# A diffusion trunk on one core: the convolution layer's modulation maps loaded ahead in a ring, its last rows' convolution maps and centring moved earlier, and the context's squares taken about a seven-tile mean

## The chip, the cores and the metric

The kernel runs on one core of a Trainium2 chip. The metric is the time in microseconds (us) of one execution on the device. Five engines work side by side, each with its own queue in program order: PE (TensorE, matrix products), DVE (VectorE), ACT (ScalarE), POOL (GpSimd) and SP (SyncE, which here only issues transfers). A queue stops at an instruction whose operands are not there yet, and all that stands behind it stops too.

## What is computed

Two layers over 1024 latent tokens and 256 context tokens of width 1024. Layer 0 mixes tokens by a convolution module, layer 1 by attention, and each is followed by a SwiGLU network. This case is about layer 0:

```python
mod_x = silu(c) @ w_mod[i] + b_mod[i]            # six vectors: shift, scale, gate, twice
mod_c = silu(c_ctx) @ w_mod[i] + b_mod[i]
hx = rmsnorm(x, norm_g[i, 0]) * (1.0 + sc_x) + sh_x
hc = rmsnorm(ctx, norm_g[i, 0]) * (1.0 + sc_c) + sh_c

def conv_module(h, ...):                          # for hx and for hc
    u = h @ w_pw1 + b_pw1
    a, gt = split(u, 2); u = a * sigmoid(gt)
    u = depthwise_conv(u, w_dw, width 31) + b_dw
    u = silu(layernorm(u, ln_g, ln_b))            # mean and variance over 1024 features
    return u @ w_pw2 + b_pw2
```

## The kernel before

Features lie on the 128 partitions, in KT = 8 tiles; tokens lie along the free dimension, in three pieces: C (256 context tokens), L and R (512 latent tokens each). A product in full precision is made of three passes (high part times high, high times low, low times high), so a weight tile of 128x1024 is loaded (`wload`), rounded on ACT into `wh` (L142), and its remainder `wl` is made by DVE (L146) or by POOL (L148), as the number `lo_dve` says.

**The beginning.** `build` first needs 16 of the modulation vectors (shift and scale, 8 feature tiles each). `mod_pe(f)` (L234) loads map f, 512 KB, on SP's queue, multiplies it on PE by silu(c) and silu(c_ctx) (L243, 8 products in two passes each, so a pair of maps is 32 rows of the trace), copies the result out on ACT (L246), transposes it (L248) and adds a bias on ACT (L250). The loop over k = 0..7 makes maps k and 8+k and then lets the generators `gC`, `gL`, `gR` go on by a step. Each of these squares the 8 tiles of its piece (ACT L388/L391, DVE L392), forms the row statistic (PE L368, DVE L334 to L342, PE L380) and applies norm, scale and shift tile by tile (DVE L400, ACT L405, DVE L406). The maps lie in ten slots `raws`, in tiles T4, T5 and KB; R's result later takes T4 and T5. Also in this loop: the loads of x for L and R (`load_x`), the row of c, c_ctx for all partitions (`cond_row`, 1 MB, and a silu of 128x2048 on ACT), and the first two weight tiles of `pw1`.

**The middle.** For k = 0..7 `pw1` makes u for the three pieces (L453 to L455, 48 products each) and gates it (L461, L462). `conv` treats 64 groups of 16 channels, q = 8k+g, each as nine products with Toeplitz maps (L531 to L534). `conv_maps` makes the two halves of a group's map on DVE (L505, 128x640 each) into a ring of slots `self.cw` (3, later 6). `modg` is `mod_dve`: the other 24 modulation vectors as reductions on DVE (L273, two for each), a step at two of three turns of the `pw1` loop.

**The end.** After the last `pw1` the remaining groups run. A group's result is taken out by ACT (L535) and DVE (L537); `conv_sum` (L557) adds up 8 groups for the mean. For the last feature tile the results go into the context's buffer by eight transfers of 16 partitions, issued from ACT (L542). Then `ln("C")`: `mean` (DVE L568, PE L570), subtract the mean from the 8 tiles (L592), square and add up (L391, L392), statistic, scale (L604), silu (L607), and the context's `pw2` (L626).

Order on each engine: the program gives a priority to every instruction, and a scheduler at build time fixes each queue.

Of the kernel before, what the change touches and what calls it, by code (L numbers as in the profile page):

```python
# [8 lines left out]
F32 = mybir.dt.float32  # L9
F32R = mybir.dt.float32r  # L10
I32 = mybir.dt.int32
AF = mybir.ActivationFunctionType
ALU = mybir.AluOpType
# [41 lines left out]
class Kern:  # L55
# [175 lines left out]
        self.col = [[{} for s in range(2)] for l in range(2)]  # L231


    def mod_pe(self, f, raw=None, rows=None):  # L234

        nc = self.nc
        out = self.bank("md")
        if raw is None:
            raw = self.raw()
        nc.sync.dma_start(raw, self.a["wmod"][f])  # L240
        with self.later(20):
            for k in range(KT):
                nc.tensor.matmul(out[0:2, 0:P], lhsT=self.cs[:, k, :], rhs=raw[:, k * P:(k + 1) * P],  # L243
                                 start=k == 0, stop=k == KT - 1)
        rows = self.sm(P) if rows is None else rows
        nc.scalar.copy(rows[0:2, :], out[0:2, 0:P])  # L246
        with self.later(40):
            nc.tensor.transpose(out[:, P:P + 2], rows[0:2, :], self.c["ident"][0:2, 0:2])  # L248
        for s in range(2):
            nc.scalar.activation(self.mod[0][s][:, f:f + 1], out[:, P + s:P + s + 1], AF.Identity,  # L250
                                 bias=self.c["bmod"][:, 0, f:f + 1], scale=1.0)
# [258 lines left out]
    def conv(self):  # L510

        nc, c = self.nc, self.c
        for q in range(KT * CG):
# [23 lines left out]
            nc.vector.tensor_tensor(v[:, g, :], v[:, g, :], o[:, OW:2 * OW], op=ALU.add)  # L537
            if g == CG - 1:
                for d, o0, nn in ((self.vc, 0, NC_), (self.vl, 2 + NC_, NL)):
                    if k == KT - 1 and d is self.vc:  # L540
                        for j in range(CG):
                            nc.scalar.dma_start(self.cvs["C"][16 * j:16 * j + 16, k, :], v[:, j, :NC_])  # L542
                    else:
                        nc.scalar.dma_start(d[k].rearrange("g q n -> q g n"), v[:, :, o0:o0 + nn])
                if k == KT - 1:
                    self.load_cv("L", k)
                    self.load_cv("R", k)

                self.conv_sum(v[:, CG // 2:] if k == KT - 1 else v, k)
            elif k == KT - 1 and g == CG // 2 - 1:  # L550
                self.conv_sum(v[:, :CG // 2], k)
            yield

    def conv_sum(self, v, k):
# [3 lines left out]
        if k:  # L558
            nc.vector.tensor_tensor(self.vsum, self.vsum, r, op=ALU.add)

    def mean(self, b):

        nc = self.nc
        ps = self.bank("st")
        if b == "C":
            m = self.sm(CTX)
            mv, shape = m.rearrange("p (s n) -> p s n", n=NC_), [P, PH, NC_]
            nc.vector.tensor_tensor(mv, self.vsum[:, :NC_].unsqueeze(1).to_broadcast(shape),  # L568
                                    self.c["selp"].unsqueeze(2).to_broadcast(shape), op=ALU.mult)
            nc.tensor.matmul(ps[:, :CTX], lhsT=self.c["ones"].to_broadcast([P, P]), rhs=m, start=True, stop=True)  # L570
            return ps
        nn, o, s0 = {"L": (NL, 2 + NC_, 0), "R": (NL, 2 + NC_, 4)}[b]
        for i in range(4):
            nc.tensor.matmul(ps[:, i * nn:(i + 1) * nn], lhsT=self.c["selp"][:, s0 + i:s0 + i + 1].to_broadcast([P, P]),
                             rhs=self.vsum[:, o:o + nn], start=True, stop=True)
        return ps
# [6 lines left out]
    def ln(self, b, stags, box):  # L583

        nc, c = self.nc, self.c
        c0, c1 = PIECES[b]
        n = c1 - c0
        cv = self.cvs[b]
        mean = self.mean(b)[:, :n]
        acc = self.acc(n)  # L590
        for k in range(KT):
            nc.vector.tensor_tensor(cv[:, k, :], cv[:, k, :], mean, op=ALU.subtract)  # L592
            self.sq_acc(acc, cv[:, k, :], k)
            yield
        pb = self.stat(acc, n)
        if b == "C":
            s = self.T(stags[0], [P, KT, n])
            box.append(s)
        else:
            shi, slo = self.halves(*stags, n)  # L600
            box.append((shi, slo))
        for k in range(KT):
            z = cv[:, k, :]
            nc.vector.scalar_tensor_tensor(out=z, in0=z, scalar=c["lng"][:, k:k + 1], in1=pb,  # L604
                                           op0=ALU.mult, op1=ALU.mult)
            if b == "C":
                nc.scalar.activation(s[:, k, :], z, AF.Silu, bias=c["lnb"][:, k:k + 1], scale=1.0)  # L607
                yield
                continue
            nc.scalar.activation(z, z, AF.Silu, bias=c["lnb"][:, k:k + 1], scale=1.0)  # L610
            self.split(shi[:, k, :], slo[:, k, :], z)
            yield
# [361 lines left out]
    def build(self):  # L974
# [20 lines left out]
            col[("sh", 0)] = self.mod[0][s][:, 0:8]  # L995
        raws = [self.T(t, [P, 4, 1024]) for t in ("T4", "T5")] + [self.T("KB", [P, 2, 1024])]
        raws = [raws[i][:, j] for j in range(4) for i in range(3) if j < raws[i].shape[1]]
        for k in range(KT):
            if k == 5:
                self.pre += [self.wload(a["pw1"][0]), self.wload(a["pw1"][KT])]  # L1000
            self.mod_pe(k, raws[2 * k % len(raws)])
            self.mod_pe(8 + k, raws[(2 * k + 1) % len(raws)])
            for s in range(2):
                nc.vector.scalar_tensor_tensor(out=self.col[0][s][0][:, k:k + 1], in0=self.mod[0][s][:, 8 + k:9 + k],
                                               scalar=1.0, in1=c["ng"][:, 0, 0, k:k + 1], op0=ALU.add, op1=ALU.mult)
            if k == 0:
                for _ in range(KT + 1):
                    next(gC)
            if k == 1:
                load_x("L")  # L1010
                self.cond_row(cr)
                for _ in range(KT + 1):
                    next(gL)
                next(gC)
            if k:
                next(gC)
                next(gL)
            if k == 3:
                xs["R"] = self.T("HS", [P, KT, 512])
                load_x("R")  # L1020
                gR = self.norm_in(0, None, (None, "T4", "T5"), *PIECES["R"], hs["R"], xt=xs["R"])
            if k > 3:
                for _ in range(2):
                    next(gR)
        for g in (gC, gL, gR):
            for _ in g:
# [19 lines left out]
        for o, n in ((0, 2), (2 + NC_, 2), (UW - 2, 2)):  # L1046
            nc.gpsimd.memset(self.U[:, :, o:o + n], 0.0)
        modg = self.mod_dve(range(16, 40), cr, (mraw, None), self.ps[:, 5:7].rearrange("p a b -> p (a b)"))
        nc.sync.dma_start(self.craw, a["wwin"][0])
        self.conv_maps()  # L1050
        cg = self.conv()
        for k in range(KT):
            for i, _ in enumerate(self.pw1(k, hs)):
                if k and i == 2:
                    self.split_u(k - 1)
                if k == KT - 1 and i == 4:
                    cw = self.T("T1", [P, 6, NM * P], F32R)
                    self.more_maps([(cw[:, 2 * j], cw[:, 2 * j + 1]) for j in range(3)])
                if 12 * k + i >= 22 and i % 3 != 1:
                    next(cg)  # L1060
                if i % 3 != 2:
                    next(modg, None)
        nc.scalar.activation(self.tiny([P, 16], "nv")[:, :1], c["ones"], AF.Silu)
        for _ in range(4):
            next(cg)
        for g0 in (0, CG // 2):
# [298 lines left out]
```

## Time and profile before

| | us |
|---|---|
| median of three runs | 3011.56 (3008.32 to 3013.97) |
| profiled execution | 3016.96 |
| its span, first to last instruction | 3015.1 |
| PE busy in the span | 2910.9 (97%) |
| DVE, ACT, POOL busy | 1894.4, 1198.0, 246.6 |
| mean granted TensorE clock | 0.982 |

The time of a run is some 2 us longer than the span of its profile. PE is busy nearly throughout, so what matters is where it is not: the first 110 us and the stretch from 363 to 411 us, which are the beginning and the end of the convolution layer.

### The profile page before, as it was taken

The page shows a single profiled execution, that of the slowest core. Times are in us where ns is not written, and L with a number is a line of the kernel's source. Part 1 is how long each engine was busy: PE and PEld are TensorE (multiplying, and loading weights), DVE is VectorE, ACT ScalarE, POOL GpSimd, SP SyncE. Part 2 cuts the span into 40 slices and gives each one's busy share as a digit, 9 for nine tenths or more (in the row PEclk, how much of TensorE's full clock was granted, in tenths as well). Part 3 has the DMA queues.
Part 4 walks back from the last instruction along what each step waited for, and adds up shares of the span by engine and source line. Part 5 has one row for each costly group of instructions (what it writes and reads, how often), then busy time and mean ns, then how long its engine had stood idle before and what let it go on. Part 6 is the DMA issues. An engine that isn't in the chain of part 4 may idle for free. (4 is left out here: it accounts for less than half of the span.)

```text
span 3015.1 us, 39080 instructions
## 1 busy us (share of the span) xinstructions
PE 2910.9 (97%) x15008; PEld 2423.4 (80%) x15008; DVE 1894.4 (63%) x3326; ACT 1198.0 (40%) x1965; POOL 246.6 (8%) x391
## 2 busy tenths in 40 slices
PE   7899979999999999999999999999999999999997
PEld 5788868888888888888888787777787778788886
DVE  5887688856556368333577899666666654743335
ACT  5222256522222235222345788645555543332222
POOL 0000001101022011000013111100000010100000
PEclk9999989999999999999989999989999999999998
DMA  6543344334355234333345211313212243443232
GB/s 238 145 122 82 85 139 140 140 123 141 103 174 187 63 119 152 100 98 98 128 149 154 81 48 45 103 68 88 79 60 81 66 136 98 147 140 97 92 98 63
DMA packets 132299, 336.89 MB, mean 112 GB/s; under 512 B 31504, under 2 KB 53008, under 8 KB 130960
## 3 DMA queue, kind: packets, MB, share of 16 engines
q1 hardware_dynamic: 76432, 221.94, 23.1%
q0 software_dynamic: 29568, 104.36, 10.6%
q10 hardware_dynamic: 26112, 8.10, 1.1%
q8 instruction: 118, 1.93, 0.3%
q14 instruction: 69, 0.57, 0.1%
HBM read 289.76 MB, written 39.19 MB: 109 GB/s over the span
## 5 line engine op out<-in xcount | busy, mean ns | idle before, releaser
L172 PE MATMUL ps<-T,wl 128*128 128x512 f32 (+1 forms) x2032 | 767.6, 378 | 8.4 <-DVE wl L146 8.4
L170 PE MATMUL ps<-T,wh 128*128 128x512 f32 (+1 forms) x2032 | 770.2, 379 | 4.2 <-ACT T L159 2.8
L171 PE MATMUL ps<-T,wh 128*128 128x512 f32 (+1 forms) x1984 | 748.5, 377 | 0.2 <-DVE T L162 0.2
L142 ACT CAST wh<-wr 128x1024 fp32r<-128x1024 f32 x285 | 299.2, 1050 | 766.9 <-PE ps L171 544.2
L146 DVE TENSOR_TENSOR wl<-wr,wh 128x1024 fp32r<-128x1024 f32 x277 | 339.0, 1224 | 295.6 <-ACT wh L142 291.8
L172 PEld LDWEIGHTS ps<-T,wl 128*128 128x128 f32 x2032 | 385.0, 189 | 79.2 <-DVE wl L146 9.7
L170 PEld LDWEIGHTS ps<-T,wh 128*128 128x128 f32 x2032 | 385.1, 190 | 73.1 <-ACT T L159 3.9
L171 PEld LDWEIGHTS ps<-T,wh 128*128 128x128 f32 x1984 | 376.0, 190 | 66.7 <-DVE T L162 1.2
L171 PE MATMUL ps<-HS,wh 128*128 128x512 f32 (+1 forms) x768 | 297.3, 387 | 0.0
L921 DVE TENSOR_TENSOR T<-ps,T 128x512 fp32r<-128x512 f32 x320 | 216.9, 687 | 110.4 <-ACT T L920 109.2
L172 PE MATMUL ps<-HS,wl 128*128 128x512 f32 (+1 forms) x720 | 279.3, 388 | 0.0
L170 PE MATMUL ps<-HS,wh 128*128 128x512 f32 (+1 forms) x720 | 278.9, 389 | 0.0
L920 ACT CAST T<-ps 128x512 fp32r<-128x512 f32 x320 | 185.9, 585 | 193.8 <-PE ps L917 178.4
L917 PE MATMUL ps<-cst,T 128*128 128x128 f32 x1100 | 192.3, 276 | 2.8 <-DVE T L921 2.7
L905 DVE TENSOR_SCALAR_CACHE_REDUCE T<-ps,rq 128x1280 f32<-128x1280 f32 x110 | 170.0, 1545 | 28.5 <-PE ps L899 24.0
L752 DVE TENSOR_TENSOR T<-ps,T 128x512 f32<-128x512 f32 (+1 forms) x168 | 110.6, 664 | 113.1 <-PE ps L172 112.4
L917 PEld LDWEIGHTS ps<-cst,T 128*128 128x128 f32 x1100 | 134.0, 142 | 49.9 <-DVE T L921 29.6
L907 ACT ACTIVATE T<-T,mn 128x1280 f32<-128x1280 f32 x110 | 150.4, 1367 | 56.3 <-DVE T L905 54.4
L727 DVE TENSOR_TENSOR sm<-sm,ps 128x256 f32<-128x256 f32 (+1 forms) x88 | 54.6, 620 | 181.2 <-PE ps L172 181.1
L171 PEld LDWEIGHTS ps<-HS,wh 128*128 128x128 f32 x768 | 144.5, 188 | 28.0 <-DVE HS L162 0.2
L172 PEld LDWEIGHTS ps<-HS,wl 128*128 128x128 f32 x720 | 135.5, 188 | 27.0
L170 PEld LDWEIGHTS ps<-HS,wh 128*128 128x128 f32 x720 | 135.1, 188 | 25.8 <-ACT HS L159 0.8
(240 smaller groups left out, 4678.5 us busy)
## 6 DMA issues: line engine op xcount, KB each, us to landing
wr<-in_w SPq DMA_DIRECT2D x220, 512.0 KB, 3.5
q<-in_w SPq DMA_DIRECT2D x44, 512.0 KB, 3.4
wr<-in_pw SPq DMA_DIRECT2D x35, 512.0 KB, 3.6
HR<-in_wmodT POOLq DMA_DIRECT2D x56, 256.0 KB, 3.9
q<-in_wmodT POOLq DMA_DIRECT2D x56, 256.0 KB, 4.0
q<-qsd POOLq DMA_DIRECT2D x32, 256.0 KB, 3.2
wr<-in_wo SPq DMA_DIRECT2D x16, 512.0 KB, 3.4
qsd<-T POOLq DMA_DIRECT2D x14, 512.0 KB, 3.8
```

What stands on the lines that cost most here:

```text
L142: nc.scalar.copy(hi, raw)
L146: nc.vector.tensor_tensor(lo, raw, hi.bitcast(F32), op=ALU.subtract)
L170: nc.tensor.matmul(out[:, :n], lhsT=wh, rhs=xh, start=k == 0, stop=False)
L171: nc.tensor.matmul(out[:, :n], lhsT=wh, rhs=xl, start=False, stop=False)
L172: nc.tensor.matmul(out[:, :n], lhsT=wl, rhs=xh, start=False, stop=k == nk - 1)
L727: nc.vector.tensor_tensor(h, sa, pb[:, :n], op=ALU.mult)
L752: nc.vector.tensor_tensor(yd, out[:, :c1 - c0], yd, op=ALU.add)
L905: nc.vector.tensor_scalar(out=pt, in0=sc, scalar1=rq[:, h:h + 1], scalar2=None, op0=ALU.mult, op1=ALU.min, accum_out=mn)
L907: nc.scalar.activation(pt, pt, AF.Exp, bias=mn, scale=-1.0, accum_out=sums[:, 0, h:h + 1])
L917: nc.tensor.transpose(tp[:, h * P:(h + 1) * P], Ps[h][:, j * P:(j + 1) * P], c["ident"])
L920: nc.scalar.copy(ph, tp)
L921: nc.vector.tensor_tensor(pl, tp, ph.bitcast(F32), op=ALU.subtract)
```

## The change

- **Maps.** Of the ten slots all are loaded before the loop (after six of them the x of L); inside it each `mod_pe` is followed by the load of the map ten places on. `cond_row` and the loads of `pw1`'s first tiles move to k = 3, `cond_row` behind the x of R. Each generator goes on at other turns. `lo_dve = 1.0` is set before the loop, so POOL makes no remainder here.
- **Middle.** The first taps for `conv_maps` are loaded once R's normalised piece is complete (a copy of one column makes the transfer wait for it). `modg` starts at k = 1.
- **End.** In the last `pw1`, from turn 8 on, three more map slots in T2 (9 in all) and a `conv_maps` at each turn. Transfers of the last tile go out on SP's queue. `shift` estimates the context's mean from seven feature tiles, and `centre` subtracts it from these and adds up their squares during the last groups; when the eighth tile is there, only the small rest of the mean is formed, its square times the number of features is subtracted from the sum of squares, and the rest is subtracted from the tiles. `conv_sum` of the last tile goes in parts of 4, 2 and 2 groups.

```diff
-    def mod_pe(self, f, raw=None, rows=None):
+    def mod_pe(self, f, raw, rows=None):
...
-        nc.sync.dma_start(raw, self.a["wmod"][f])
...
                 for d, o0, nn in ((self.vc, 0, NC_), (self.vl, 2 + NC_, NL)):
+                    eng = nc.sync if k == KT - 1 else nc.scalar
...
-                            nc.scalar.dma_start(self.cvs["C"][16 * j:16 * j + 16, k, :], v[:, j, :NC_])
+                            eng.dma_start(self.cvs["C"][16 * j:16 * j + 16, k, :], v[:, j, :NC_])
...
-                self.conv_sum(v[:, CG // 2:] if k == KT - 1 else v, k)
-            elif k == KT - 1 and g == CG // 2 - 1:
-                self.conv_sum(v[:, :CG // 2], k)
+                self.conv_sum(v[:, CG - 2:] if k == KT - 1 else v, k)
+            elif k == KT - 1:
+                if g == 0:
+                    sh = self.shift()
+                for _ in range(2):
+                    next(sh, None)
+                for g0, g1 in ((0, CG // 2), (CG // 2, CG - 2)):
+                    if g == g1 - 1:
+                        self.conv_sum(v[:, g0:g1], k)
...
+    def by_token(self, v):
+        nc = self.nc
+        ps = self.bank("st")
+        m = self.sm(CTX)
+        mv, shape = m.rearrange("p (s n) -> p s n", n=NC_), [P, PH, NC_]
+        nc.vector.tensor_tensor(mv, v.unsqueeze(1).to_broadcast(shape),
+                                self.c["selp"].unsqueeze(2).to_broadcast(shape), op=ALU.mult)
+        nc.tensor.matmul(ps[:, :CTX], lhsT=self.c["ones"].to_broadcast([P, P]), rhs=m, start=True, stop=True)
+        return ps[:, :CTX]
+
+    def shift(self):
+        nc, cv = self.nc, self.cvs["C"]
+        self.part = self.tiny([P, NC_], "part")
+        nc.vector.tensor_scalar(out=self.part, in0=self.vsum[:, :NC_], scalar1=KT / (KT - 1.0), scalar2=None,
+                                op0=ALU.mult)
+        self.about = self.by_token(self.part)
+        self.cacc = self.acc(CTX)
+        for k in range(KT - 1):
+            self.centre(k)
+            yield
+
+    def centre(self, k):
+        cv = self.cvs["C"][:, k, :]
+        self.nc.vector.tensor_tensor(cv, cv, self.about, op=ALU.subtract)
+        self.sq_acc(self.cacc, cv, k)
...
+        if b == "C":
+            acc, dist = self.cacc, self.tiny([P, NC_], "dist")
+            nc.vector.tensor_tensor(dist, self.vsum[:, :NC_], self.part, op=ALU.subtract)
+            mean = self.by_token(dist)
+            self.centre(KT - 1)
+            sq = self.sb(n)
+            nc.scalar.activation(sq, mean, AF.Square, scale=(D / P) ** 0.5)
+            nc.vector.tensor_tensor(acc, acc, sq, op=ALU.subtract)
...
+        def load_map(i):
+            if i < 2 * KT:
+                nc.sync.dma_start(raws[i % len(raws)], a["wmod"][i % 2 * KT + i // 2])
+        for i in range(len(raws)):
+            if i == 6:
+                load_x("L")
+            load_map(i)
+        self.lo_dve = 1.0
         for k in range(KT):
-            if k == 5:
-                self.pre += [self.wload(a["pw1"][0]), self.wload(a["pw1"][KT])]
-            self.mod_pe(k, raws[2 * k % len(raws)])
-            self.mod_pe(8 + k, raws[(2 * k + 1) % len(raws)])
+            for i in (2 * k, 2 * k + 1):
+                self.mod_pe(i % 2 * KT + k, raws[i % len(raws)])
+                load_map(i + len(raws))
...
-            if k == 1:
-                load_x("L")
-                self.cond_row(cr)
+            if k == 2:
...
             if k == 3:
+                self.pre += [self.wload(a["pw1"][0]), self.wload(a["pw1"][KT])]
                 xs["R"] = self.T("HS", [P, KT, 512])
                 load_x("R")
                 gR = self.norm_in(0, None, (None, "T4", "T5"), *PIECES["R"], hs["R"], xt=xs["R"])
+                self.cond_row(cr)
             if k > 3:
-                for _ in range(2):
+                for _ in range(3 if k < 6 else 2):
                     next(gR)
...
+        nc.vector.tensor_copy(self.craw[:, 0:1], hs["R"][0][1][:, KT - 1, 0:1].bitcast(F32))
         nc.sync.dma_start(self.craw, a["wwin"][0])
...
+                if k == KT - 1 and i >= 8:
+                    if i == 8:
+                        cw = self.T("T2", [P, 6, NM * P], F32R)
+                        self.more_maps([(cw[:, 2 * j], cw[:, 2 * j + 1]) for j in range(3)])
+                    self.conv_maps()
...
-                if i % 3 != 2:
+                if k and i % 3 != 2:
                     next(modg, None)
```

What the change does to the queues, at three places (line numbers of the changed kernel are larger; the operations are told by their tiles).

**SP, the beginning.** `in_wmod` is a map, T_113, T_114 and KB its slots, `in_xT` into T_106 the x of L and into HS the x of R, `in_crow` the row for `cond_row`, `in_pw` a weight tile of `pw1`. Before:

```order
L987 DMA T_106<-in_xT 128x2x512 x4
L254 DMA HR<-in_crow 128x2048
L240 DMA T_114<-in_wmod 128x1024
L240 DMA KB<-in_wmod 128x1024
L240 DMA T_113<-in_wmod 128x1024
L240 DMA T_114<-in_wmod 128x1024
L987 DMA HS<-in_xT 128x2x512 x4
L240 DMA T_113<-in_wmod 128x1024
L240 DMA T_114<-in_wmod 128x1024
L141 DMA wr_74<-in_pw 128x1024
```

Now, from the fourteenth map on:

```order
L1036 DMA T_113<-in_wmod 128x1024
L1036 DMA T_114<-in_wmod 128x1024
L1036 DMA KB<-in_wmod 128x1024
L141 DMA wr_74<-in_pw 128x1024
L141 DMA wr_73<-in_pw 128x1024
L1022 DMA HS<-in_xT 128x2x512 x4
L251 DMA HR<-in_crow 128x2048
L141 DMA wr_74<-in_pw 128x1024
```

All 16 maps now stand ahead of `pw1`'s tiles, of R's x and of the row; before, the last eight stood behind R's x and six of them behind `pw1`'s tiles too.

**ACT, around the last pair of maps.** `mod` adds the bias to the last map's product, `q<-KB` rounds the first taps, `sb<-HS` squares R, `HR<-HR` is the silu of the row, `wh` rounds a weight tile, T_274 and T_283 (before) or T_204 and T_325 (now) are the normalised C and L. Before:

```order
L250 ACTIVATE mod_101<-ps,cst 128x1
L250 ACTIVATE mod_102<-ps,cst 128x1
L391 ACTIVATE sb<-HS 128x512
L405 ACTIVATE T_274<-sb,mod_102 128x256
L405 ACTIVATE T_283<-sb,mod_101 128x512
L391 ACTIVATE sb<-HS 128x512
L159 CAST q<-KB 128x320
```

Now:

```order
L247 ACTIVATE mod_101<-ps,cst 128x1
L247 ACTIVATE mod_102<-ps,cst 128x1
L402 ACTIVATE T_204<-sb,mod_102 128x256
L388 ACTIVATE sb<-HS 128x512
L402 ACTIVATE T_325<-sb,mod_101 128x512
L388 ACTIVATE sb<-HS 128x512
L252 ACTIVATE HR<-HR 128x2048
L142 CAST wh<-wr_74 128x1024
L402 ACTIVATE T_204<-sb,mod_102 128x256
L402 ACTIVATE T_325<-sb,mod_101 128x512
```

The row's silu and the rounding of the third weight tile now stand between the last pair of maps and the last tile of C; before, the silu stood far ahead of this place, and the first taps were rounded right behind it.

**DVE, the end of the convolution.** HR gets a group's result, `sm<-HR` is `conv_sum`, KB the context's buffer, `acc` its squares. Before, from the last groups to the statistic:

```order
L537 TENSOR_TENSOR HR<-HR,ps 128x162 x4
L557 TENSOR_REDUCE sm<-HR 128x162
L559 TENSOR_TENSOR HR<-HR,sm 128x162
L568 TENSOR_TENSOR sm<-HR,cst 128x256
L592 TENSOR_TENSOR KB<-KB,ps 128x256 x4
L392 TENSOR_TENSOR acc<-acc,sb 128x256
L592 TENSOR_TENSOR KB<-KB,ps 128x256
```

Now:

```order
L534 TENSOR_TENSOR HR<-HR,ps 128x162 x2
L561 TENSOR_REDUCE sm<-HR 128x162
L563 TENSOR_TENSOR HR<-HR,sm 128x162
L616 TENSOR_TENSOR dist<-HR,part 128x32
L571 TENSOR_TENSOR sm<-dist,cst 128x256
L590 TENSOR_TENSOR KB<-KB,ps 128x256
L389 TENSOR_TENSOR acc<-acc,sb 128x256
L626 TENSOR_TENSOR KB<-KB,ps 128x256
L621 TENSOR_TENSOR acc<-acc,sb 128x256
L626 TENSOR_TENSOR KB<-KB,ps 128x256 x7
L370 TENSOR_SCALAR nv<-ps 128x2
```

Of the eight squares only one is left behind the last group; the eight subtractions are still there, and now stand ahead of the statistic's first row (`nv`). The first `by_token` product stands in PE's queue inside the second group of the last tile.

## Rows read from the trace of the kernel before

**Rows 1.** Stretches of the beginning: from:to in us, its length, then busy us (and instructions) of PE, PE's weight loads, DVE, ACT and POOL, the granted clock, DMA share, GB/s.

```profile
23.00:36.00 13.00, 9.40 (x46) 6.15 (x46) 6.95 (x24) 5.14 (x10) 0.00 (x0) 0.61 1.04 398
91.00:99.40 8.40, 5.76 (x24) 4.36 (x24) 7.17 (x12) 1.73 (x2) 0.00 (x0) 1.00 0.42 125
99.40:106.60 7.20, 6.42 (x27) 5.73 (x28) 5.71 (x9) 0.41 (x1) 0.00 (x0) 0.54 0.85 228
```

**Rows 2.** What PE waited for in the first 440 us: its line, the work that released it, us in total, times, the longest.

```profile
PE ps L243 <- DMA T<-in_wmod: 10.9, 1, 10.9
PE ps L368 <- DVE acc L392: 7.9, 2, 5.6
PE ps L531 <- DVE HR L537: 6.3, 5, 2.8
PE ps L570 <- DVE sm L568: 4.0, 1, 4.0
```

**Rows 3.** PE in order of time: start, us, line, operation, count, and in brackets the idle time before it and what ended it. L243 are the maps, L453 to L455 the products of `pw1`.

```profile
10.93 5.45 PE L243 MATMUL ps<-T,cs 128*2 128x128 f32 x32 [10.93 <-DMA T<-in_wmod]
...
36.70 3.66 PE L243 MATMUL ps<-T,cs 128*2 128x128 f32 x32
...
41.01 3.65 PE L243 MATMUL ps<-T,cs 128*2 128x128 f32 x32
...
48.28 5.32 PE L243 MATMUL ps<-T,cs 128*2 128x128 f32 x32
...
61.64 1.91 PE L243 MATMUL ps<-KB,cs 128*2 128x128 f32 x16
...
90.90 0.50 PE L453 MATMUL ps<-T,wh 128*128 128x512 f32 x1 [1.02 <-DVE HR L462]
...
96.37 0.39 PE L455 MATMUL ps<-T,wl 128*128 128x512 f32 x1
99.41 0.39 PE L453 MATMUL ps<-T,wh 128*128 128x256 f32 x1 [2.65 <-ACT wh L142]
```

**Rows 4.** Transfers of the first 112 us: GB/s in 40 equal slices of 2.8 us, then SP's issue of R's x (start, us), then the longest wait of SP's queue for PE (at L1049, the first taps).

```profile
GB/s 42 343 353 409 391 399 417 405 399 388 390 408 411 407 413 130 4 200 180 0 0 0 0 246 6 59 18 29 0 0 0 0 0 187 187 92 254 219 310 70
...
17.40 5.54 SPq L987 DMA_DIRECT2D HS<-in_xT  x4
...
SPq L1049 <- PE ps L248: 14.0, 1, 14.0
```

**Rows 5.** ACT and DVE in order of time in the beginning: the row's silu, the rounding of a weight tile, a square of R, a remainder, and two runs of R's application.

```profile
26.43 1.89 ACT L255 ACTIVATE HR<-HR 128x2048 f32<-128x2048 f32 x1
43.40 1.03 ACT L142 CAST wh<-wr 128x1024 fp32r<-128x1024 f32 x1
61.90 0.61 ACT L391 ACTIVATE sb<-HS 128x512 f32<-128x512 f32 x1
84.99 2.06 DVE L400 SCALAR_TENSOR_TENSOR sb<-HS,col,ps 128x512 f32<-128x512 f32 x3
86.96 2.07 DVE L406 SCALAR_TENSOR_TENSOR T<-sb,mod,T 128x512 fp32r<-128x512 f32 x3
100.10 1.22 DVE L146 TENSOR_TENSOR wl<-wr,wh 128x1024 fp32r<-128x1024 f32 x1
```

**Rows 6.** The loop over k: when DVE gates R's piece for k = 0, 1 and 7 (L462), and two stretches of one k's length, with and without `modg` (columns as in Rows 1).

```profile
98.30 0.75 DVE L462 SCALAR_TENSOR_TENSOR HR<-ps,cst,sm 128x512 f32<-128x512 f32 x1
...
135.68 0.74 DVE L462 SCALAR_TENSOR_TENSOR HR<-ps,cst,sm 128x512 f32<-128x512 f32 x1
...
364.22 0.75 DVE L462 SCALAR_TENSOR_TENSOR HR<-ps,cst,sm 128x512 f32<-128x512 f32 x1 [1.86 <-ACT sm L461]
...
139.00:177.00 38.00, 38.00 (x226) 34.10 (x225) 33.56 (x51) 8.36 (x15) 0.00 (x0) 1.00 0.46 125
300.00:338.00 38.00, 38.00 (x225) 34.10 (x224) 22.64 (x35) 7.62 (x14) 0.00 (x0) 1.00 0.24 54
```

**Rows 7.** PE at the end of the convolution, in order of time: two groups back to back, a group after a wait, the last group's last product, the mean (L570), the statistic (L368).

```profile
364.55 0.31 PE L531 MATMUL ps<-HS,T 128*128 128x324 f32 x1
...
365.85 0.31 PE L531 MATMUL ps<-HS,T 128*128 128x324 f32 x1
...
386.32 0.42 PE L531 MATMUL ps<-HS,T 128*128 128x324 f32 x1 [2.77 <-DVE HR L537]
...
394.35 0.35 PE L534 MATMUL ps<-HS,T 128*128 128x324 f32 x1
398.66 1.22 PE L570 MATMUL ps<-sm,cst 128*128 128x256 f32 x2 [3.96 <-DVE sm L568]
405.45 1.01 PE L368 MATMUL ps<-cst,acc 128*128 128x1 f32 x4 [5.57 <-DVE acc L392]
```

**Rows 8.** DVE at the end: busy us and count of map halves (L505) in one stretch, then in order of time the sum over eight groups, the sum over four, the last squares, and the context's scaling (L604).

```profile
364.80:398.20 33.40, 15.69 (x20) 0.93 0.66 189
...
382.57 2.49 DVE L557 TENSOR_REDUCE sm<-HR 128x162 f32<-128x1296 f32 x1
...
390.37 1.35 DVE L557 TENSOR_REDUCE sm<-HR 128x162 f32<-128x648 f32 x1
...
403.91 1.48 DVE L392 TENSOR_TENSOR acc<-acc,sb 128x256 f32<-128x256 f32 x3
...
409.61 3.22 DVE L604 SCALAR_TENSOR_TENSOR KB<-KB,cst,ps 128x256 f32<-128x256 f32 x8 [0.78 <-PE ps L380]
```

More of the change, by code (lines that the diff above doesn't have):

```diff
@@ L231, in consts @@
         self.col = [[{} for s in range(2)] for l in range(2)]
-    def mod_pe(self, f, raw=None, rows=None):
+    def mod_pe(self, f, raw, rows=None):
         nc = self.nc
         out = self.bank("md")
-        if raw is None:
-            raw = self.raw()
-        nc.sync.dma_start(raw, self.a["wmod"][f])
         with self.later(20):
@@ L539, in conv @@
                 for d, o0, nn in ((self.vc, 0, NC_), (self.vl, 2 + NC_, NL)):
+                    eng = nc.sync if k == KT - 1 else nc.scalar
                     if k == KT - 1 and d is self.vc:
                         for j in range(CG):
-                            nc.scalar.dma_start(self.cvs["C"][16 * j:16 * j + 16, k, :], v[:, j, :NC_])
+                            eng.dma_start(self.cvs["C"][16 * j:16 * j + 16, k, :], v[:, j, :NC_])
                     else:
-                        nc.scalar.dma_start(d[k].rearrange("g q n -> q g n"), v[:, :, o0:o0 + nn])
+                        eng.dma_start(d[k].rearrange("g q n -> q g n"), v[:, :, o0:o0 + nn])
                 if k == KT - 1:
@@ L564, in mean @@
         ps = self.bank("st")
[L565 to L571, printed above, removed]
         nn, o, s0 = {"L": (NL, 2 + NC_, 0), "R": (NL, 2 + NC_, 4)}[b]
@@ L588, in ln @@
         cv = self.cvs[b]
-        mean = self.mean(b)[:, :n]
-        acc = self.acc(n)
+        if b == "C":
[6 more added lines that the diff above has]
+            nc.vector.tensor_tensor(acc, acc, sq, op=ALU.subtract)
+        else:
+            mean = self.mean(b)[:, :n]
+            acc = self.acc(n)
         for k in range(KT):
             nc.vector.tensor_tensor(cv[:, k, :], cv[:, k, :], mean, op=ALU.subtract)
-            self.sq_acc(acc, cv[:, k, :], k)
+            if b != "C":
+                self.sq_acc(acc, cv[:, k, :], k)
             yield
@@ L1008, in build @@
                     next(gC)
-            if k == 1:
-                load_x("L")
-                self.cond_row(cr)
+            if k == 2:
                 for _ in range(KT + 1):
                     next(gL)
-                next(gC)
-            if k:
-                next(gC)
+            next(gC)
+            if k >= 2:
                 next(gL)
             if k == 3:
+                self.pre += [self.wload(a["pw1"][0]), self.wload(a["pw1"][KT])]
                 xs["R"] = self.T("HS", [P, KT, 512])
@@ L1058, in build @@
                     self.more_maps([(cw[:, 2 * j], cw[:, 2 * j + 1]) for j in range(3)])
+                if k == KT - 1 and i >= 8:
[3 more added lines that the diff above has]
+                    self.conv_maps()
                 if 12 * k + i >= 22 and i % 3 != 1:
                     next(cg)
-                if i % 3 != 2:
+                if k and i % 3 != 2:
                     next(modg, None)
         nc.scalar.activation(self.tiny([P, 16], "nv")[:, :1], c["ones"], AF.Silu)
+        self.banks["st"], self.ring["st"] = [6, 5], 0
         for _ in range(4):
```

## The prediction, made before the changed kernel was run

> **What bounds the kernel now.** I read the shares of busy time first: PE is busy in 97% of the span, so only its waits and its slow stretches can be won. PE's waits of the first 440 us [rows 2] name the places: 10.9 us until the first map lands, and later waits for DVE around the norms, the groups and the mean. The stretches [rows 1] add the clock: from 23 to 36 us PE was busy for 9.4 of 13.0 us at a granted 0.61, a mixture of the levels 1.2 and 2.4 GHz, after idle stretches; from 99.4 to 106.6 it was 0.54, after the 2.65 us in which PE had nothing to do because the weights for k = 1 came late [rows 3]. PE's order in time [rows 3] shows the maps' course: a pair starts at 36.70 and the next at 41.01, so 4.31 us a pair at full clock (3.66 of products, the rest transposes and copies); at the lower level the products of a pair take 5.32. The last map ends near 63.5, with `pw1` products laid between the pairs, and the first R piece ends near 96.7. Transfers run at about 400 GB/s up to 42 us and then nearly stop [rows 4]: the early stretch is filled by bytes that are not all wanted first.
>
> The loop over k is full: R's piece is gated at 98.30, 135.68 and 364.22 us [rows 6], so six k from 1 to 7 take 228.5, 38.1 each. A group costs 1.30 [rows 7], eight are 10.4 to 10.5, so `pw1` itself is 27.6 for one k. The first step of the loop, 98.30 to 135.68, took 37.4 with only one group in it, 28.9 of work: 8.5 were lost there.
>
> At the end, PE has 16 groups left at 363.2, which are 21 us of work, but ends them at 394.7 [rows 7], behind DVE, which makes 20 map halves there for 15.69 us [rows 8] beside gating, splitting and sums. Then the context's mean, squares and statistic run one after another while PE waits 3.96 and 5.57 us [rows 7]; the context's scaling starts at 409.61 [rows 8].
>
> **The change, part by part.** *Maps first.* Ahead of the last map now stand the constants (0.2 MB), C's x (1.05), 16 maps (8.4) and L's x (2.1), 11.8 MB; at the rate of [rows 4] that is some 33 us. PE takes longer: the first pair as before from 10.93 to 16.4, then seven pairs at 4.31 make 46.6, and two norms' statistics and transposes between them about 2, so the last map is through at 48.5, 15 us earlier than now.
>
> A rule of the Trainium skill speaks against the ring: DMA: Bandwidth & Descriptors, in the section on the anatomy of one DMA, says that the engines that move data do not wait on semaphores, so that a transfer's wait is done by the sequencer that issues it; the load of a slot's second map would hold everything behind it on SP. The row agrees: SP stood 14.0 us at L1049 for PE [rows 4]. By that rule the sixteenth map can be issued when the sixth is through, at 27.0 by the pairs above, and R's x, issued at 17.40 before [rows 4], behind it; with 3.7 MB behind that point it lands by 42, or by 44 if the pairs run slower. ACT's queue comes to R's squares at about 47.5 either way; a longer stop of SP is rival (d).
>
> *From the last map to the end of the first R piece.* PE then has 27.6 us of k = 0 and 15 products of C for k = 1 (1.8) in its queue: 77.9 if nothing waited. ACT's queue decides what waits. Between 44 and 59 us it has the two roundings (1.03 each), eight squares of R (0.61), the small copies and biases of the last two pairs, applications for C and L, and then, as the order shows, the row's silu (1.89) and the third rounding [rows 5] ahead of C's last tile. DVE then makes a remainder (1.22) [rows 5], two applications, and R's statistic, which takes 3.2 with its transposes (for the context it is 406.46 to 409.61 [rows 7, 8]); all that ends near 64.9. PE waits there about 2, and about 4 in small pieces before. R's application, with the last two tiles of L and a gating, follows on DVE: 21 instructions at 0.69 (six in 84.99 to 89.03 [rows 5]) up to 79.4; then 23 products of R are left, at 0.24 (24 from 90.90 to 96.77 [rows 3]), 5.4: R ends at 84.8. Before it ended at 96.8. **12 us gained**; bounds: 18 if no wait is left, 4 if all pairs from the fourth run at 1.2 GHz (five times 1.66).
>
> *k = 1.* Its weights are rounded at 59, long before they are needed, and POOL's remainder (PE waited for it) is DVE's now, at 1.22, hidden by the norms. The 8.5 us lost now shrink to about 1, and 1.8 were already done: **9 us gained**; bounds 6 and 10.
>
> *k = 2 to 7.* `modg` leaves k = 0 and is in k = 6. DVE is busy 33.6 of 38 with it and 22.6 without [rows 6]: the eight steps fit. In k = 1 and 2 DVE gets the first maps too, and is filled to about 37 of 38. **0**, bounds 2 either way. Without that cover each microsecond of DVE over PE's 38.1 would count in full.
>
> *The end.* DVE has 14 map halves behind the last gating instead of 20, 0.78 each, 4.7 us less; but `centre` puts five subtractions and as many sums, the first product of a scaled sum, and a reduction of its own before the last group. The first `by_token` product stands in PE's queue inside a group; it needs the sum over k = 6's groups (2.49 [rows 8]) and two short steps, so PE stands there for some 3 to 4 us, where before it stood for 2.77 at about the same work [rows 7]. Counted through DVE's queue from the last gating (364.9 before), the last group ends 28.2 later instead of 29.8. Then the reduction is over two groups, half of the 1.35 for four [rows 8]; ACT's issues of the eight transfers are gone from between its outputs. The mean's product goes off at 31 instead of 33.8. Of the squares one is left, not eight: the sum is ready 2.4 after the product starts, not 6.8; but the eight subtractions, 2.4 more, stand ahead of the statistic, as the order shows. Statistic and transposes as before. The scaling starts at 38.9 instead of 44.7: **6 us gained**; bounds 0, if PE's stop costs the rest of the groups, and 9, if the subtractions hide under the statistic's product. Beyond this place the queues are those of before but for a few rows where attention starts, which I count as 0, one either way.
>
> Sum: 12 + 9 + 0 + 6 = 27. The profiled execution's 3016.96 would be 2990. It stood 5.4 above the median of the runs shown, so the median goes from 3011.56 to **2984.5**. A tenth of a per cent either way is the runs' own scatter; below 0.2% (6 us) I call it no change.
>
> **The rivals.** (a) *The lower clock in the pairs.* From 23 to 36 us the clock fell after short idle stretches; the ring feeds PE without gaps, but copies on ACT still stop it 0.2 to 0.6 us at each pair. If five pairs run at 1.2 GHz, 8 us of the 12 go: 2993. TensorE: Matmul & The Clock Gate, in the section on what is actually happening, in the Trainium skill, has the lower level as the default that activity lifts; the first pair's 5.45 agrees [rows 3].
>
> (b) *The tail moves its wait.* PE's stop inside the last tile, followed by groups at a lower clock, takes all 6: 2990. For it: the groups after 386.32 did start slowly.
>
> (c) *More at the beginning.* If ACT's chain is shorter than I read it, R's application starts with the transfers' end and PE is full from 48.5 on, and the tail gives 9: 18 + 10 + 9 = 37, so 2975.
>
> (d) *The change doesn't do what it says.* SP, stopped by the ring, delivers R's x and `pw1` so late that R ends where it did. For that R's application would have to start 15 us later than I count, with x landing after 57; the bytes speak against it. Then only part of the end is left: 3008.
>
> (e) *Slower: DVE binds the convolution.* `modg` moved into k = 1 to 6 lies on maps, splits and sums. From 33.6 us a k it would have to rise over 38.1 + 27/6 = 42.6 to eat the gain; at 44 the time is 3020. Against it, the same steps lay on the same work before for k = 2 to 5 without a wait of PE.
>
> **How the numbers follow.** My forecast has 0.60, (a) 0.14, (b) 0.10, (c) 0.08, (d) 0.04, (e) 0.04. The bounds of the terms give gains from 10 to 37; dropping the corners, and with the runs' scatter, the range is 2969 to 3001; it holds (a), (b) and (c). Faster 0.92, the same 0.04, slower 0.04.
>
> **What would show it.** Right: the last map's product ends between 46 and 52 and the pairs follow at 4.3; R's gating for k = 0 between 82 and 90, for k = 1 about 27 later, and from there 38.1 a k to the last; no wait of over 2 us for `wh` near 100; 14 map halves after the last gating; a wait of 3 to 4 us of PE for DVE at the first `by_token`; the context's scaling some 39 after the last gating. Wrong: pairs of 5.3, an SP wait for PE that moves R's x beyond 47, waits for maps or for group outputs in k = 1 to 6, or a stop of PE at the end longer than the squares saved.

## The result, and the profile after

The changed kernel takes 2995.03 us (median of 6, 2989.61 to 3000.7) against 3014.41 for the kernel before on the same chip: ratio 0.9938, 95% interval 0.9927 to 0.995, some 19 us. Beside the last experiments it was timed once more: 0.9929 (0.9917 to 0.9941). Its profiled execution took 2998.7, 18.3 less than the one before.

PE's waits in the first 440 us, as in [rows 2]:

```profile
PE ps L240 <- DMA T<-in_wmod: 9.6, 1, 9.6
PE ps L573 <- DVE sm L571: 5.9, 2, 3.5
PE ps L377 <- DVE nr L339: 5.0, 4, 3.5
PE ps L450 <- DVE HR L459: 2.8, 3, 1.9
PE ps L528 <- DVE HR L534: 2.4, 2, 1.6
PE ps L365 <- DVE acc L621: 1.9, 1, 1.9
```

The wait for the squares is 1.9 where it was up to 5.6; L573 (`by_token`) now stops PE twice. Three stretches (columns as in [rows 1]): 23 to 36 us, where the clock was 0.61, and the place where R's statistic is awaited:

```profile
23.00:36.00 13.00, 11.40 (x99) 8.52 (x97) 10.68 (x33) 7.88 (x24) 0.00 (x0) 1.00 1.03 406
...
60.00:66.00 6.00, 4.49 (x14) 3.25 (x15) 4.88 (x18) 2.01 (x4) 0.00 (x0) 0.62 0.32 92
66.00:72.00 6.00, 6.00 (x23) 4.75 (x22) 6.00 (x10) 3.31 (x5) 0.00 (x0) 0.81 0.14 18
```

The last map, then R's gating for k = 0, 1 and 7, to be held against [rows 3, 6]:

```profile
47.98 1.91 PE L240 MATMUL ps<-KB,cs 128*2 128x128 f32 x16
...
88.59 0.75 DVE L459 SCALAR_TENSOR_TENSOR HR<-ps,cst,sm 128x512 f32<-128x512 f32 x1
...
115.33 0.74 DVE L459 SCALAR_TENSOR_TENSOR HR<-ps,cst,sm 128x512 f32<-128x512 f32 x1
...
345.89 0.75 DVE L459 SCALAR_TENSOR_TENSOR HR<-ps,cst,sm 128x512 f32<-128x512 f32 x1 [1.80 <-ACT sm L458]
```

They lie 9.7, 20.4 and 18.3 us earlier. The end on PE, to be held against [rows 7]: the two `by_token` products, the statistic, its transposes (L377), the first `pw2`:

```profile
366.46 1.22 PE L573 MATMUL ps<-sm,cst 128*128 128x256 f32 x2 [3.50 <-DVE sm L571]
...
377.78 0.35 PE L531 MATMUL ps<-HS,T 128*128 128x324 f32 x1
380.55 0.70 PE L573 MATMUL ps<-sm,cst 128*128 128x256 f32 x2 [2.41 <-DVE sm L571]
383.12 1.02 PE L365 MATMUL ps<-cst,acc 128*128 128x1 f32 x4 [1.87 <-DVE acc L621]
387.68 0.69 PE L377 MATMUL ps<-cst,nr 128*128 128x128 f32 x2 [3.54 <-DVE nr L339]
```

And the same transposes before:

```profile
408.88 0.69 PE L380 MATMUL ps<-cst,nr 128*128 128x128 f32 x2 [2.42 <-DVE nr L342]
```

So 21.2 are gained here, and 20.6 are still there at a statistic near 2567 us (2588.24 before). Most of what is then lost down to 18.3 is lost at a place that the change does not edit: behind the wait for that statistic PE ran at a granted 0.50 and 0.74 for 8 us in this execution, and at 1.00 in another of the same kernel (last section).

### The profile page after: what moved, and what is told of

Same layout as the page of the kernel before. It is cut to its first block, busy times and chain, and to the rows that moved or that the text cites. A ratio compares the mean times of both kernels' runs of the same rounds, so it can differ in the third digit from the quotient of the medians.

```text
span 2996.7 us, 39100 instructions
## 1 busy us (share of the span) xinstructions
PE 2905.9 (97%) x15010; PEld 2422.1 (81%) x15010; DVE 1901.1 (63%) x3343; ACT 1195.8 (40%) x1964; POOL 241.8 (8%) x389
## 3 DMA queue, kind: packets, MB, share of 16 engines
q8 instruction: 118, 1.93, 0.3%
## 5 line engine op out<-in xcount | busy, mean ns | idle before, releaser
L172 PEld LDWEIGHTS ps<-T,wl 128*128 128x128 f32 x2032 | 385.0, 190 | 79.9 <-DVE wl L146 9.8
```

The lines of the kernel that those rows point to most:

```text
L172: nc.tensor.matmul(out[:, :n], lhsT=wl, rhs=xh, start=False, stop=k == nk - 1)
```

## The experiments

The change has three parts that can be done alone: the **ring** (maps first, the norms' new turns), the **late modg** (`if k and`) and the **tail**. Profiles differ in when the first map lands (8.2 to 10.9 us), so R's gatings are counted from PE's first map product. The column of us is what the ratio makes of 3014 us; the last column is the distance from the last gating to the statistic's transposes.

| kernel | ratio to before (95%) | us | gating k = 0 | k = 1 | k = 7 | to transposes |
|---|---|---|---|---|---|---|
| before | 1 | 0 | 87.4 | 124.8 | 353.3 | 44.7 |
| e7 ring | 0.9986 (0.9975 to 0.9997) | -4 | 80.0 | 120.5 | 349.8 | 44.6 |
| e9 late modg | 0.9963 (0.9951 to 0.9975) | -11 | 85.7 | 115.1 | 342.1 | 44.9 |
| e2 tail | 0.9993 (0.9982 to 1.0003) | -2 | 86.9 | 123.5 | 350.2 | 41.1 |
| e10 ring, late modg, no copy | 0.9957 (0.994 to 0.9973) | -13 | 80.1 | 108.7 | 336.0 | 44.7 |
| e1 ring, late modg, copy | 0.9951 (0.9936 to 0.9966) | -15 | 79.9 | 107.4 | 338.1 | 45.3 |
| e6 ring, copy, tail | 0.9955 (0.9941 to 0.997) | -14 | 80.0 | 115.0 | 342.5 | 40.2 |
| change | 0.9938 (0.9927 to 0.995) | -19 | 79.0 | 105.7 | 336.3 | 41.8 |
| e5 change, POOL | 0.9943 (0.9923 to 0.9962) | -17 | 79.6 | 106.3 | 339.6 | 40.2 |

**The tail taken away (e1), and alone (e2).** The old `conv_sum`, `mean` and squares of C, ACT for the last transfers, no slots in T2; or these alone put into the kernel before.

```diff
-                        cw = self.T("T2", [P, 6, NM * P], F32R)
...
-        if b == "C":
-            acc, dist = self.cacc, self.tiny([P, NC_], "dist")
...
+        mean = self.mean(b)[:, :n]
+        acc = self.acc(n)
```

> The change without its last part: the context's mean and squares, the sums of the last tile, its transfers' queue and the map slots are those of before; the maps' ring and the middle are those of the change. In the trace of the change the context's scaling starts 21.2 us earlier than before, the last gating 18.3 earlier, so the last part looks worth 2.9 there. Theory 1 (2.9 is what it is worth to the end): the change loses 3 us, about 2998. Theory 2, the prediction's size (6 us): 3001. Theory 3 (the tail's gain is given back later, since the whole kernel ended only 18.3 earlier): the same as the change, 2995 with 1 us either way.

> The kernel before with only the last part of the change. Theory 1: 3 us faster than before, 3011.5; in the trace the distance from the last gating to the context's scaling falls from 45.4 to about 42.5. Theory 2 (the prediction's 6): 3008.5, distance 39. Theory 3: no difference, whatever the distance. In all of them the first 345 us are those of before, the last gating at about 364.

Against the change, e1 loses 4 us (by the two ratios; 7 against the change's second timing), with intervals that overlap, and e2 gains 2 on the kernel before; the distances fall by 3.5 and 3.6. In the traces that is Theory 1, some 3 us; the times agree with it, but are too coarse to show it. Six lies outside e2's interval, which ends at 5.4; no gain at all does not.

**modg in k = 0 again (e6), the ring alone (e7), the late modg alone (e9), the ring without the copy (e10).**

```diff
 e6, e7:
-                if k and i % 3 != 2:
+                if i % 3 != 2:
 e7, e10 (both also without the tail, as e1):
-        nc.vector.tensor_copy(self.craw[:, 0:1], hs["R"][0][1][:, KT - 1, 0:1].bitcast(F32))
 e9, in the kernel before:
-                if i % 3 != 2:
+                if k and i % 3 != 2:
```

> The change with the reductions of modg started in k = 0 again. In the trace of the change k = 1 to 7 takes 230.6 us from the first to the last gating of R, before it took 228.5. Theory 1 (shifting modg freed DVE for R's application, which is what lets PE go on without the pieces of waiting at 80 to 91 us): the gating for k = 0 comes 3 to 6 us later, PE waits for DVE's applications again, k = 1 to 7 falls back by 1 to 2; in all about 2998. Theory 2 (the shift of modg costs the 2 us in k = 1 to 7 and gains nothing): about 2993. Theory 3: no effect on the sum, 2995.

> Only the maps' ring and the new turns of the norms (with the remainders on DVE): modg begins in k = 0, the first taps are loaded without waiting for R's piece, and the whole last part is that of before. Theory 1 (the ring itself is the gain): the last map is through at 49 to 50 as in the change, the gating for k = 0 lies at 89 to 93, for k = 1 some 28 to 30 later, and the kernel takes 2997 to 3002. Theory 2 (ring and late modg are both needed): the last map as in the change, but R's gating for k = 0 at 95 or later, and 3006 or more.

> The kernel before with one edit: modg begins in k = 1. With the ring and modg in k = 0 the third weight tile of pw1 was issued on SP at 85.2 us, behind modg's rows, and rounded at 90.8; in the change it was issued at 46.0 and rounded at 57.9. Theory 1 (modg's rows ahead of pw1's tiles on SP's queue cause the loss at k = 1, with or without the ring): the third tile is rounded before 70 us, PE's wait of 2.65 us for it near 99 is gone, the step from the first to the second gating of R falls from 37.4 to 28 to 31, and the kernel takes 3003 to 3007. Theory 2 (the shift is of use only behind the ring): the wait moves to R's application, and the time is that of before within 2 us.

> The ring, with modg from k = 1, the whole last part as before, and the first taps loaded without waiting for R's piece (the copy of one column is left away). The same with the copy took 2997.8. Theory 1 (the copy only keeps the taps' load out of the way and costs or gains nothing): 2998, the second gating of R at about 116. Theory 2 (the early taps let DVE make convolution maps between R's applications, which delays them): the first gating of R 2 to 5 us later and 3001 to 3003.

These four decide the case. The ring alone brings the first gating forward by 7.4 us, to within 1 us of the change's, but 3.1 are lost again in the step to k = 1 (40.5 us, before 37.4). PE in e7, at the first product of k = 1 that waits:

```profile
91.85 0.58 PE L450 MATMUL ps<-T,wh 128*128 128x256 f32 x1 [4.20 <-ACT wh L142]
```

What SP issued, and into which slots, says why. Its issues in e7, start and us; L264 are modg's rows, L141 the weight tiles of `pw1`, L1053 the taps:

```profile
48.89 0.34 SPq L1053 DMA_DIRECT2D KB<-in_wwin  x1
49.27 0.43 SPq L264 DMA_DIRECT2D KB<-in_wmodT  x1
49.80 0.86 SPq L264 DMA_DIRECT2D wr<-in_wmodT  x2
...
81.45 0.34 SPq L264 DMA_DIRECT2D KB<-in_wmodT  x1
85.21 0.33 SPq L141 DMA_DIRECT2D wr<-in_pw  x1
```

And what SP waited for in e7 between 40 and 100 us (total, times, longest):

```profile
SPq L264 <- DVE mod L270: 19.8, 2, 17.0
SPq L1053 <- PE ps L245: 14.6, 1, 14.6
...
SPq L141 <- DVE mod L270: 4.1, 2, 3.3
```

The last reduction by which DVE reads the first of the two rows in `wr`, in e7:

```profile
83.90 1.23 DVE L270 CUSTOM_DVE_ANT_0 ps<-wr,HR 128x1024 f32<-128x1024 f32 x1
```

In the change, at the same place:

```profile
46.03 2.51 SPq L141 DMA_DIRECT2D wr<-in_pw  x2
49.91 0.33 SPq L264 DMA_DIRECT2D KB<-in_wmodT  x1
60.75 0.33 SPq L264 DMA_DIRECT2D wr<-in_wmodT  x1
```

And in e9, which has no ring; then the gating of R for k = 0 and 1 there, and the stretch between the two (columns as in [rows 1]):

```profile
46.26 2.66 SPq L141 DMA_DIRECT2D wr<-in_pw  x2
...
94.64 0.75 DVE L462 SCALAR_TENSOR_TENSOR HR<-ps,cst,sm 128x512 f32<-128x512 f32 x1 [0.35 <-ACT sm L461]
...
124.05 0.74 DVE L462 SCALAR_TENSOR_TENSOR HR<-ps,cst,sm 128x512 f32<-128x512 f32 x1
...
94.64:124.05 29.41, 29.39 (x156) 25.48 (x157) 20.48 (x30) 6.41 (x8) 0.00 (x0) 1.00 0.57 174
```

With modg in k = 0 the two slots `wr`, into which weight tiles land, go to modg's rows at 49.80, and the next row (81.45) waits 17.0 for DVE, with the next `pw1` tile behind it on SP. The tile then waits 3.3 more for its own slot, whose row DVE has read only at 85.1, behind R's application; it is issued at 85.21 and rounded at 90.8. So the slot, and not the queue, was the last to hold the tile. With modg a step later the two tiles themselves are issued, at 46.03 (the change) or 46.26 (e9), and the first of them is rounded at 57.9 or 57.5. In the kernel before SP did as in e7: rows into `wr` at 46.88, the tile at 94.72, the 2.65 us of [rows 3]. Theory 1 of e9 held: that one line is worth 11 us alone (3001.95 measured, 3003 to 3007 expected), and the step from k = 0 to 1 is 29.4. In that step PE's waits fell from 4.3 us, of which 2.7 for `wh` and 1.1 for its remainder, to 0.8, and the clock, 0.54 behind the wait in [rows 1], was 1.00 throughout. The line also takes modg's reductions out of DVE's work in k = 0; no run moved the rows to slots of their own, so what the reductions alone cost is not separated, but PE's long waits were for the weights. Neither theory on e7 stood as worded: the first gating came as the first said, the time as the second, since the loss comes behind that gating. That a transfer's wait is done by the engine that issues it is the rule of the Trainium skill that the prediction cites (DMA: Bandwidth & Descriptors, in the section on the anatomy of one DMA). The trace agrees: SP itself stood 17.0 and 3.3 us for DVE. What counted here were these two waits, not the ring's waits for PE, of which the longest in the change was 1.5.

In e6 the step to k = 1 takes 35.0 where the change takes 26.7. Of its three theories the first has the time (2998.1), but not the place: the first gating is only 1.1 later, and the loss lies behind it. Beside the ring, the copy and the tail the late modg is thus worth 5 to 8 us (e6 against the change's two timings, with intervals that overlap or touch), and 9 on the ring alone (e10 against e7). e10 shows the copy to be worth nothing that can be measured once modg is late (0.9957 beside 0.9951); e7's step of 40.5 us against e6's 35.0 suggests that it helps while modg is early, but the two differ in the tail too, so that stays open.

**The remainders on POOL again (e5).**

```diff
-        self.lo_dve = 1.0
         for k in range(KT):
```

> The change with the remainders of the first two weight tiles made by POOL, as before, and not by DVE. In the change DVE makes the third tile's remainder (1.23 us from 59.50) between the sum of R's statistic (59.42) and its next step (61.70), and PE then waits 0.64 and 0.83 and runs at a clock of 0.62 from 60 to 66 us. Theory 1 (POOL stops PE): PE waits 1.5 us or more for POOL's remainder near 48 us, as it did for 1.62 before, and the gating of R for k = 0 comes 1 to 3 us later than 88.6 with the first map at 9.6; about 2997. Theory 2 (a DVE relieved of two remainders brings R's statistic earlier): gating at 87 or earlier, about 2993.

Neither: PE did not wait for POOL, and R's statistic was awaited as before (0.83 at 63.30), behind the third tile's remainder and two applications for C, which are DVE's in both kernels. The time is the change's within the interval.

**The tail's inside: without the subtractions (e3), the estimate later (e4, e8), a smaller last sum (e11), the change again (e12).**

```diff
 e3, for C only:
-            nc.vector.tensor_tensor(cv[:, k, :], cv[:, k, :], mean, op=ALU.subtract)
 e4 (e8: 3 for 2; e11: as e4, and the last group added by itself):
-                if g == 0:
+                if g == 2:
                     sh = self.shift()
-                for _ in range(2):
+                for _ in range(2 if g >= 2 else 0):
```

> The change without the eight subtractions of the small rest of the mean from the context's tiles (that part of the computation is left out). In the trace of the change they take DVE from 382.31 to 385.29, while PE's statistic, which the next DVE instruction needs, ends at about 384.1. Theory 1 (only what sticks out counts): the statistic's row starts about 1.0 us earlier and the scaling too, so 2994. Theory 2 (all their time counts): 2.4 us, 2992.6. Theory 3 (nothing at this place reaches the end): 2995.

> The change with the estimate of the mean asked for two groups later, so that its product on PE stands behind the third group of the last tile instead of inside the second. Theory 1 (PE's stop of 3.50 us at the first product, and the 5 us at a lower clock behind it, delay the last group): the stop falls to 1 us or less, the last group ends 3 to 5 us earlier against the last gating (now 32.2 behind it), and the kernel takes about 2991. Theory 2 (DVE's queue sets the groups' pace there, PE's stop only moves): another stop of PE for DVE comes in its place, the last group ends within 1 us of where it did, and the kernel takes 2995 with 1 us either way.

> The change with the estimate of the mean asked for three groups later, so that its product stands on PE behind the fourth group of the last tile. With two groups later the first stop was 1.71 us, the second 3.42, and the transposes of the statistic came 38.5 us after the last gating (change: 41.8). Theory 1 (the first stop goes altogether, the rest stays): about 37 us after the last gating, 1 to 1.5 us faster than with two groups. Theory 2 (the centring of seven tiles then crowds the last groups on DVE): the second stop grows by what the first loses, 38.5 us and the same time, 2991.

> The change with the estimate of the mean two groups later, and the last tile's sums in parts of 4, 3 and 1 groups, the last of which is added without a reduction. With the shift alone the transposes of the statistic came 38.5 us after the last gating of R, and the kernel took 2991.6. Theory 1 (the last reduction, 0.49 us, and one step between it and the sum lie on the path): 0.5 to 0.9 us earlier, 37.7, too little to be seen in the time: 2991. Theory 2 (the reduction over three groups then stands in front of the last group's output): no gain, 38.5 or more.

> The change itself once more, beside the others of this chip: 0.994 of the kernel before, with the transposes of the statistic 41.8 us after the last gating of R. If the difference to the two kernels with a later estimate of the mean is real, it is 3 to 4 us slower than they are.

| | ratio (95%) | us, median | stop at the 1st and 2nd `by_token` | last gating to transposes |
|---|---|---|---|---|
| e12 change again | 0.9929 (0.9917 to 0.9941) | 2994.0 | 3.49, 2.42 | 41.7 |
| e3 | 0.9926 (0.9911 to 0.994) | 2992.4 | 3.49, 2.42 | 40.2 |
| e4 | 0.9924 (0.9911 to 0.9937) | 2991.6 | 1.71, 3.42 | 38.5 |
| e8 | 0.9929 (0.991 to 0.9947) | 2994.9 | below 0.5, 4.36 | 39.1 |
| e11 | 0.9919 (0.9907 to 0.9931) | 2990.1 | 1.72, 1.93 | 38.5 |

The last column alone does not give the cost of the subtractions: e5 and e6, whose tail is the change's, have 40.2 there too. Counted from the second `by_token` product, the transposes come 5.95 us later in e3, and 7.1 to 7.2 in the change, e2, e5, e6 and e12. So the subtractions cost 1.2 of their 2.4 us in the trace, near Theory 1 of e3; the times do not tell its theories apart. For e4 the stretches of the change, then of e4, from 350 us on (columns as in [rows 1]):

```profile
362.70:366.40 3.70, 0.26 (x2) 0.06 (x1) 3.56 (x6) 0.40 (x1) 0.00 (x0) 0.85 0.95 271
366.40:372.00 5.60, 5.54 (x21) 5.37 (x22) 4.11 (x14) 2.62 (x8) 0.00 (x0) 0.50 0.65 188
372.00:378.20 6.20, 6.13 (x46) 5.90 (x45) 4.96 (x12) 2.03 (x7) 0.00 (x0) 0.99 0.19 49
```

```profile
362.70:366.40 3.70, 1.99 (x13) 1.71 (x13) 3.56 (x7) 1.08 (x3) 0.00 (x0) 1.00 1.01 264
366.40:372.00 5.60, 5.60 (x44) 5.48 (x43) 5.54 (x15) 2.56 (x8) 0.00 (x0) 1.00 0.54 164
372.00:378.20 6.20, 2.35 (x11) 1.40 (x9) 4.38 (x13) 1.82 (x6) 0.00 (x0) 0.75 0.24 62
```

In the change PE does two products in 3.7 us and then runs for 5.6 us at half speed (0.50, the lower level of 1.2 GHz), so 21 products instead of 44. In e4, at full clock, the last group ends 27.5 us after the last gating instead of 32.2; 1.0 comes back at the second stop. That is Theory 1 in place, though the first stop is still 1.71. Its size is 3.3 us against this profile of the change and 1.7 against e5 and e6. These two have the change's tail and the same first stop (3.49), but over the 9 us behind it the clock was 0.81, and the last group ended 10.6 us after the stop; in the change it was 0.69 and 11.7 us, in e12 0.64 and 12.1. So, with no edit at this place, the length of the slow stretch alone moves the last group by 1.0 to 1.4 us. In e8 Theory 2 holds in place: PE stops for 1.94 at a group and for 4.36 at the second product instead, and the time is 2994.9. In e11 too: the second stop shrinks to 1.93, but the last group ends 28.9 after the last gating, not 27.5. In time e4 and e11 have the lowest medians of all, 3 to 4 us under the change on paper; against e12, on its chip, the intervals of e11 still overlap, so the end-to-end gain is likely and not shown.

## Why the prediction was right, and where not

The time was within the range, the sum 27 against 19 measured. In the two profiles, counted from the first map, the four steps gave 8.4 + 10.6 - 2.1 + 2.9 = 19.8 where the prediction had 12 + 9 + 0 + 6. By its steps:

- **Maps first, 12 us.** Right in kind, with no wait of SP that mattered. The first gating gained 8.4 from the first map on (7.4 by the ring alone), not 12. Of the 3.6 that lack, 2.7 lay ahead of the last map: it was through at 49.9 (48.5 forecast), though the first had landed 1.3 earlier. The pairs came 4.3 apart from the fifth on, but the second to the fifth, with the statistics of two norms between them, 5.5 apart, and the working had 4.31 for each and 2 us for both norms. Behind the last map the working was nearly right in sum, and not by its terms: PE stood for 1.9 us, not 6, but it ran at 0.62 and 0.81 from 60 to 72 us behind two short waits (0.64 for a tile of C, 0.83 for R's statistic), which the working did not price, and 173 `pw1` products stood ahead of that gating, not the 159 that it had (144 and 15), so that some of k = 1's work was done earlier. No run separates these three. Rival (a) went the other way: the ring held the clock up between 23 and 36 us, and the maps' products on PE fell from 36.5 to 32.3 us. The groups of the maps by tile up to R's first gating, before and then in the change (busy us, mean ns, idle before):

```profile
L243 PE MATMUL ps<-T,cs 128*2 128x128 f32 x192 | 27.9, 309 | 11.1 <-DMA T<-in_wmod 10.9
L243 PE MATMUL ps<-KB,cs 128*2 128x128 f32 x64 | 8.6, 292 | 0.0
```

```profile
L240 PE MATMUL ps<-T,cs 128*2 128x128 f32 x192 | 24.7, 287 | 9.8 <-DMA T<-in_wmod 9.6
L240 PE MATMUL ps<-KB,cs 128*2 128x128 f32 x64 | 7.6, 273 | 0.1
```

- **k = 1, 9 us.** The step was 26.7, as said (about 27), and the saving 10.6. The sign that the prediction named, the early rounding, was the right one; its cause was not among the costs. The step that failed is the one on k = 2 to 7: "`modg` leaves k = 0 and is in k = 6" was priced at 0 by DVE's work, without the transfers that it issues on SP and the slots that they hold. By e9 that edit is worth 11 us by itself, more than any other, and by e7 the ring without it is worth 4. The prediction took the early rounding from the changed queues without asking which part of the change brings it; that the step came out right is luck to that extent.
- **k = 2 to 7, 0.** 230.6 against 228.5 in this profile, at the bound of 2; over all profiles 227.0 to 233.3 with a late modg and 226.6 to 229.4 with an early one, so a cost of 1 or 2 is likely and small beside their scatter. DVE was filled to 35.9 of 40.4 us in k = 2 and held; rival (e) is out.
- **The end, 6 us.** 14 map halves (11.03 us) and a stop of 3.5 us at the first `by_token`, as forecast. The step that failed is "the last group ends 28.2 later". Counted as there, from the end of the last gating, it ended at 31.5 (29.8 before), because groups behind the stop ran at half the clock. The mean's product went off at 33.9, where 31 was forecast and 33.8 had been, so nothing was gained ahead of it; the squares behind it gave the forecast 3.0, and the scaling started at 41.8, not 38.9. That was rival (b)'s mechanism, which was to take all 6; it took about half. The transposes came 2.9 earlier (3 to 4.5 over the other profiles). With the stop shortened (e4) the group ended at 26.8.
- **Rivals (c) and (d)** fell: the gain is 19, not 37, and R's x arrived in time. The total came out in the range because the late modg's gain stood, by its effect, under the name of k = 1.

## What to carry to other kernels

When a background step moves, list its transfers and the buffers that they occupy, not only its time on the engine that works it off: here two weight slots decided over 11 us alone, and over 5 to 8 of the 19 beside the other parts. A part that brings a stage forward is paid only if the next stage's operands come forward too. A product placed in PE's queue before its operand can be there costs the stop and, here, slow products behind it. Two groups later the stop was half as long (1.71 us) and no slow stretch followed it; what that gains end to end is not shown.

## What the runs showed of the chip that was not expected

The clock after a short stop is not the same from one execution to the next. Near 2567 us PE waits for the same statistic in every profile, for 1.6 to 3.4 us. In the profiled execution of the change and in e12, the same kernel, the wait is:

```profile
2567.59 1.12 PE L377 MATMUL ps<-cst,nr 128*128 128x128 f32 x4 [3.29 <-DVE nr L339]
```

```profile
2566.07 0.65 PE L377 MATMUL ps<-cst,nr 128*128 128x128 f32 x4 [2.75 <-DVE nr L339]
```

In the 4 us behind it the clock was 0.50 in the one and 1.00 in the other; in e1, after 2.78 us, it was 0.57. The length of the wait does not settle it: after 3.29 us, as in the first of the two, it was 0.67 in e8, and after 3.07 us 0.66 in e2. A single profile can so differ by some 3 us at a place that no edit touched, which is as much as the whole tail is worth.
